# Thin products of the triangular inverses issued in groups of four blocks, with dense products between them

## The chip, the cores and the metric

The kernel runs on one core of a Trainium2 chip. A core has engines that run beside each other, each through its own queue in order: TensorE (PE in the profile; its weight loads are shown apart as PEld), VectorE (DVE), ScalarE (ACT), GpSimd (POOL) and SyncE (SP), which here issues the DMA transfers. The metric is the device time of one execution in microseconds (us), lower is better.

## What is computed

One inference step of a hybrid layer for 1024 prompt tokens and 8 sample tokens with 1024 channels, in float32. The input is normed and projected; two token mixers run on slices of that projection; their results are merged through gates, and a SwiGLU block and a per-layer embedding follow. Cut to what matters here:

```python
u = rmsnorm(h, norm_mix)
proj = u @ w_in                               # the dense products of the first half
# mixer 1, RWKV-7: 8 heads, a state of 64 x 64 each, token by token
sa = einsum('bhvk,bhk->bhv', S, a_t)
S = S * w_t + sa[..., None] * b_t + v_t[..., None] * k_t
# mixer 2, gated DeltaNet: 4 heads, in chunks of 64 tokens
lmat = where(strict, einsum('nbhik,nbhjk->nbhij', kb, k) * decay, 0.0)
tinv = triangular_solve(eye + lmat, eye, lower=True, unit_diagonal=True)
v_new = tinv @ vb - (tinv @ (kb * exp(gc))) @ S
# afterwards
mix = gate_a * (o_a @ w_branch_a) + gate_b * (o_b @ w_branch_b)
h = h + mix @ w_out                           # then SwiGLU, the embedding, the final norm
```

The kernel runs both mixers in chunks of 64 tokens, so that both need inverses of unit triangular 64x64 blocks.

## The kernel before

**Dense products.** A weight is split into a rounded part and a rest (`wh`, `wl`: `weights`, L181; ACT rounds at L188, POOL takes the rest at L189), the activations too (`xh`, `xl`; later `oah`, `oal`, `obh`, `obl`), and each product is the sum of three: `wh*xh + wh*xl + wl*xh`. Tokens are cut into three blocks of 344, so a dense product has 128x128 weights and 344 columns. The input projection has 3360 of them (46 column tiles of 72 products, and one narrow one of 48). They come from the generator `stream` (L396), one at a time; ACT takes each finished accumulation off at L432 and SP stores it at L433.

**The order on TensorE** is written out by a planner, `order` (L112). It keeps a clock of its own, which `mm` (L74) advances by an assumed time for each product (a dense one 0.148 us, a thin one of 32 columns 0.058 us). Each piece of other work is a generator (`Task`) that yields a time by which its next products have to stand back, or marks for which they wait. In every round the first task that may go on does; when none may, one dense product of the stream is issued. When the stream is empty, the planner's clock jumps and tasks follow each other with nothing between. The other engines are ordered by the framework's scheduler.

**Thin products.** DVE inverts the 32x32 diagonal blocks; TensorE then makes the corner of each 64x64 inverse from them by two products with 32x32 weights and 32 columns. For RWKV (`rwkv_inverse`, L749) this happens eight times (4 pairs of heads, 2 halves of the prompt), with 16 blocks each: 16 products into `s` from `inv`, GM (L797), ACT copies them (L798), then 16 more from GM, `inv` (L802). Then the `chains` (L817) go on: a recurrence whose products (`c<-PB`, `zp<-X`, `zp<-Rz`) each wait for DVE. For DeltaNet (`inverses`, L1103) it happens once, after a long stretch on DVE (to L1131, for which the task stands back 54.0 us of the planner's clock), with 32 blocks of 128: `f<-AN` and `f<-tm` for the two diagonal pairs (0, 1) and (2, 3), then `f<-LT` of both pairs, and `f<-W` (L1137 to L1156), and last eight groups with 64x64 blocks. A float32 product of this kind shows as two records in the trace.

**What follows.** `steps`, `preps` and `posts` run the DeltaNet recurrence in 8 steps, again with dense products between. The last `post` scales `ob` (L1372), turns it on TensorE (`f<-cs,ob`), DVE multiplies it with the gate (L1380), and SP stores it to `ob_d` (L1381). Behind that store in SP's queue stand the loads of the first branch's input (`U<-oa_d`, L1401), which ACT and DVE split (L239, L240) for the first dense products of the next stage (`acc<-oah`). What is left of the stream is issued there (`order([], dense_in, [])`).

Of the kernel before, what the change touches and what calls it, by code (L numbers as in the profile page):

```python
# [19 lines left out]
P = 128  # L20
T = 1024
NS = 8
TOK = T + NS
NBLK = 3
BW = TOK // NBLK
# [8 lines left out]
EPS = 1e-6  # L34
# [24 lines left out]
def hybrid(ctx, tc, a, o):  # L59
# [4 lines left out]
    done = {}  # L64
    clock = [0.0]
    last = [None]
    ORDER = mybir.DependencyInfo(mybir.DependencyClass.NoSync, mybir.DependencyReason.DATA)

    def late(i):
        """Keeps an instruction behind the products traced so far, so that what it waits for is there when it is issued."""  # L70
        tc.add_manual_dep(i.ins, last[0].name, ORDER, reason="behind the products so far")
        return i

    def mm(out, w, x, start, stop):  # L74
        last[0] = TE.matmul(out, w, x, start=start, stop=stop).ins  # L75
        clock[0] += math.prod(x.shape[1:]) * (0.00042 if x.dtype == F32R else 0.0017) + 0.004
# [8 lines left out]
    class Task:  # L85
        """A generator that yields where its next products have to wait: for so long, or for marks and so long after."""

# [24 lines left out]
    def order(tasks, stream, until):  # L112
        """Traces the products of all tasks in the order in which they are to run, until those of until are done: the
        first task that can go on does, else the stream of dense products. With no tasks: the rest of the stream."""
        until = list(until)
        with tc.manual_schedule(engines={mybir.EngineType.PE}):
            if not tasks:
                for _ in stream:
                    pass
            while until:  # L120
                times = [t.ready() for t in tasks]
                t = next((t for t, r in zip(tasks, times) if r is not None and r <= clock[0]), None)
                if t is not None:
                    if not t.advance():
                        tasks.remove(t)
                        if t in until:
                            until.remove(t)
                elif next(stream, None) is None:
                    clock[0] = min(r for r in times if r is not None)
# [13 lines left out]
    def ft(shape):  # L143
        return psf.tile(shape, F32, tag="f", name="f")
# [55 lines left out]
    def dense(src, nk, xh, xl, evac):  # L200
        """Products with one column tile of a weight; what is at hand of other work goes first."""
        tc.cur_priority += LATER
        wh, wl = weights(src, nk)
        tc.cur_priority -= LATER
        products(wh, wl, nk, xh, xl, evac)
# [20 lines left out]
    def rsq(out, x, scale, eps, m, t):  # L226
        """out = (x * scale + eps)^-0.5; m, t: temporaries. Seed from the exponent, three Newton steps."""
        if x is not None:
            ts(m, x, scale, eps, MULT, ADD)
        ts(t.bitcast(I32), m.bitcast(I32), 1, None, ALU.logical_shift_right)  # L230
        ts(out.bitcast(I32), t.bitcast(I32), -1, 0x5F3759DF, MULT, ADD)
        for _ in range(3):
            tt(t, out, out, MULT)  # L233
            stt(t, t, -0.5, m, MULT, MULT)  # L234
            stt(out, t, 1.5, out, ADD, MULT)
# [8 lines left out]

    # ------------------------------------------------------------------ input norm, per-layer projection
    xstk = ExitStack()
# [11 lines left out]
    def inv_rms(R, ps, pl_, newps):  # L258
        """R = (mean + EPS)^-0.5 from the sums ps, both [P, BW] and the same on all partitions.

        The sums are taken to tokens on partitions, where there is little to compute, and the result is spread again."""
        n = ps.shape[1]
# [17 lines left out]
    with tc.tile_pool(name="ld", bufs=1, side="right", reuse_waits="tile") as ld, \  # L280
# [35 lines left out]
        def sums(g):  # L316
            """The sums of squares of one block; the squares take the place of what is split."""
            sq = (pv + [own], wv + [own], pv)[g]
# [10 lines left out]
            ps = ct([P, BW])  # L329
# [66 lines left out]
    def stream(jobs):  # L396
        """The products of the input projection, one tile of its columns after the other; yields after each product."""
        def fetch(ti):
# [54 lines left out]
    def conv(ci):  # L453
        """Short causal convolution of one tile of q, k, v, by blocks of tokens; 2 silu of it goes to c_d."""
        w = [vc("conv", j * 12 + ci) for j in range(4)]
# [47 lines left out]

    # ------------------------------------------------------------------ RWKV-7
    lstk, rstk = ExitStack(), ExitStack()
# [39 lines left out]
    def shifted(ti, raw, dst=None):  # L545
        """raw: [P, TOK + 1], column 0 the zero before the prompt; token shift, in place or to dst (chunks, samples)."""
        late(G.tensor_copy(sho[:, ti], raw[:, T:TOK + 1]))
# [161 lines left out]
    def gram(F, hf):  # L709
        """Products within the chunks of one half."""  # L710
        v, BC, KR, cvf = (F[x] for x in ("v", "BC", "KR", "cv"))
# [37 lines left out]
    def rwkv_inverse(f, hf):  # L749
        """The inverses of the triangular blocks."""  # L750
        GM = UT[f, hf]["GM"]
# [44 lines left out]
        for b in range(16):  # L796
            mm(ps[32:64, b], GM[0:32, b, 32:64], inv[0:32, b], start=True, stop=True)  # L797
        act(E, ps[32:64], AF.Copy)  # L798
        yield 1.0
        ps = st1([P, 16, 32])  # L800
        for b in range(16):
            mm(ps[0:32, b], E[:, b], GM[32:64, b, 32:64], start=True, stop=True)  # L802
        act(GM[0:32, :, 32:64], ps[0:32], AF.Copy)
        mark(("inverse", f, hf), 1.0)

    YT = {}

# [92 lines left out]
    def rwkv_sample(f, sm):  # L900
        """One step for the eight samples; partitions (head, value), free (sample, key)."""
        sm, sn = sm
# [51 lines left out]
    def branch_in(f):  # L954
        """The input of the first branch: the normed rows and the bonus, times the gate."""
        g2 = gsp.tile([P, BW], F32, tag="cu", name="g2", bufs=1)[:, :P]
# [22 lines left out]

    # ------------------------------------------------------------------ gated DeltaNet  # L980
    NB = NM * HB
# [18 lines left out]
    def decays():  # L1000
        """beta, g of all tokens (on partitions), the decay between the tokens of a chunk."""
        yield ("pa", "b"),
# [102 lines left out]
    def inverses():  # L1105
        """The inverses of the triangular blocks of all heads and chunks."""
        for m in range(NM):
# [23 lines left out]
        V.transpose(A2.rearrange("p b c -> p c b"), XT4[qd[2]])  # L1131
        yield 54.0
        PS = {}
        for q0 in (0, 16):
            bs = range(q0, q0 + 16)
            ps = ft([P, 16, 32])
            for (u, w), nat in (((0, 1), AN), ((2, 3), tm4)):  # L1137
                for b in bs:
                    mm(ps[qd[w], b - q0], LTb[qd[u], b, qd[w]], nat[qd[u], b, 0:32], start=True, stop=True)
            E = LB4[:, q0:q0 + 16]  # L1140
            for w in (1, 3):
                act(E[qd[w]], ps[qd[w]], AF.Copy)
        yield 0.9
        for q0 in (0, 16):
            bs = range(q0, q0 + 16)
            E = LB4[:, q0:q0 + 16]
            ps = ft([P, 16, 32])
            for u, w in ((0, 1), (2, 3)):
                for b in bs:
                    mm(ps[qd[u], b - q0], E[qd[w], b - q0], LTb[qd[w], b, qd[w]], start=True, stop=True)  # L1150
                act(LTb[qd[u], q0:q0 + 16, qd[w]], ps[qd[u]], AF.Copy)
            yield 0.9
            ps = ft([P, 16, 32])
            for b in bs:
                mm(ps[qd[1], b - q0], LTb[qd[1], b, qd[1]], E[qd[1], b - q0], start=True, stop=True)
            act(AN[qd[1], q0:q0 + 16, 0:32], ps[qd[1]], AF.Copy)  # L1156
# [18 lines left out]
    def gdn_sample():  # L1175
        """One step for the eight samples; partitions value, free (head, sample, key)."""
        qs_, ks_, vs_, zs_ = (smp[:, i] for i in (0, 0, 2, 3))
# [209 lines left out]

    # ------------------------------------------------------------------ branches and merge
    hU = pool(ctx, "hU", 1, "right")
# [51 lines left out]
    def square(m, b, last=False):  # L1441
        """Sum over the channel tiles of h^2; with the last tile, its mean's inverse root goes to R."""
        c = cols(b)
# [25 lines left out]

    # ------------------------------------------------------------------ SwiGLU, per-layer embedding, final norm  # L1470
    hstk = ExitStack()
# [75 lines left out]
def layout(i):  # L1547
    """The inputs in the order in which the chip reads them (transposed, cut into tiles, concatenated)."""
    i = {k: np.asarray(v) for k, v in i.items()}
# [59 lines left out]
```

## Time and profile before

| | us |
|---|---|
| median of three runs | 2112.76 |
| the three runs | 2109.33, 2112.76, 2114.94 |
| span of the profiled execution, first to last instruction | 2108.4 |
| TensorE busy in it | 1970.4 |

The profiled execution's own time is not listed apart from its span; the span lies 0.9 us under the fastest run and 4.4 us under the median. The page cuts the span into 40 slices with the busy share of each engine and TensorE's granted clock; queries give stretches, waits and single instructions. Matmuls are pipelined: the duration of one dense product (0.32 us) is twice the spacing from one start to the next, so costs are taken here from starts.

### The profile page before, as it was taken

To read this page: it belongs to the slowest core of one execution; us is meant where nothing else is said; L and a number is where in the kernel's file an instruction comes from. 1 tells how busy PE (TensorE), PEld (TensorE's weight loads), DVE (VectorE), ACT (ScalarE), POOL (GpSimd) and SP (SyncE) were. 2 spreads that over 40 slices of the span, in tenths; PEclk is the share of its full clock that TensorE was granted. 3 is DMA by queue.
4 is the path that set the end of the run, shared out by engine and by line. 5 is a ranking of instruction groups with operands and counts; after the bars stand their busy time and mean duration, and the time that the engine had idled before them with its cause. 6 is when DMAs were issued, how large, how long until landed. Compare 5 with 4: busy or idle time off the path is not lost.

```text
span 2108.4 us, 35962 instructions
## 1 busy us (share of the span) xinstructions
PE 1970.4 (93%) x13440; PEld 1872.5 (89%) x13440; DVE 1125.4 (53%) x2889; ACT 729.5 (35%) x1785; POOL 875.2 (42%) x1019
## 2 busy tenths in 40 slices
PE   6997899888898999798999999999999999999996
PEld 5987778777787879688999999999999999999995
DVE  8459757889988749727545352221222122223567
ACT  5334344455554442136623332211221121123442
POOL 5366343356464344533027433323322332333642
PEclk9998899999999999789999999999999999999998
DMA  6433233133233434554464311111111111111232
GB/s 220 131 111 110 80 96 102 56 113 102 90 113 100 140 91 138 148 154 133 135 193 135 97 54 51 46 40 57 46 41 45 55 47 38 54 49 41 67 100 97
DMA packets 171048, 195.67 MB, mean 93 GB/s; under 512 B 42968, under 2 KB 130920, under 8 KB 170872
## 3 DMA queue, kind: packets, MB, share of 16 engines
q1 hardware_dynamic: 170872, 193.36, 30.2%
q8 instruction: 106, 1.74, 0.3%
q14 instruction: 70, 0.57, 0.1%
HBM read 141.26 MB, written 52.03 MB: 92 GB/s over the span
## 4 chain that ended last, share of the span: by engine, by line
PE 52%; DVE 1%; ACT 0%; issue 0%; DVEq 0%; ACTq 0%
PE acc L75 50%; PE f L75 1%; PE x L75 1%; PE o L75 0%; PE f L79 0%; DVE fo L1529 0%; DVE U L1517 0%; DVEq L1595 0%; DVE b L1514 0%; DVE nrr L234 0%; DVE nrr L233 0%; ACT jk L1292 0%; ACT R L278 0%; DVE b L1516 0%; ACT t L1335 0%
## 5 line engine op out<-in xcount | busy, mean ns | idle before, releaser
L189 POOL TENSOR_TENSOR wl<-ws,wh 128x512 fp32r<-128x512 f32 (+2 forms) x292 | 365.1, 1266 | 645.4 <-ACT wh L188 629.1
L75 PE MATMUL acc<-uxh,wh 128*128 128x344 f32 (+2 forms) x1248 | 400.3, 321 | 0.1
L75 PE MATMUL acc<-uxl,wh 128*128 128x344 f32 (+2 forms) x1248 | 399.5, 320 | 0.0
L75 PE MATMUL acc<-uxh,wl 128*128 128x344 f32 (+2 forms) x1248 | 399.5, 320 | 0.0
L75 PE MATMUL acc<-xh,wh 128*128 128x344 f32 (+1 forms) x1128 | 388.5, 344 | 3.6 <-ACT gs L432 3.6
L75 PE MATMUL acc<-xl,wh 128*128 128x344 f32 (+1 forms) x1128 | 384.5, 341 | 1.8 <-DVE xl L243 1.8
L75 PE MATMUL acc<-xh,wl 128*128 128x344 f32 x1104 | 379.4, 344 | 0.0
L188 ACT ACTIVATE wh<-ws 128x512 fp32r<-128x512 f32 (+2 forms) x292 | 161.6, 595 | 415.7 <-PE acc L75 376.6
L75 PEld LDWEIGHTS acc<-uxh,wh 128*128 128x128 f32 x1248 | 234.9, 188 | 1.0 <-DVE b L1514 0.4
L75 PEld LDWEIGHTS acc<-uxh,wl 128*128 128x128 f32 x1248 | 234.9, 188 | 0.6
L75 PEld LDWEIGHTS acc<-uxl,wh 128*128 128x128 f32 x1248 | 234.3, 188 | 0.7
L75 PEld LDWEIGHTS acc<-xh,wh 128*128 128x128 f32 (+1 forms) x1128 | 220.3, 195 | 11.8 <-ACT gs L432 3.9
L75 PEld LDWEIGHTS acc<-xl,wh 128*128 128x128 f32 (+1 forms) x1128 | 220.7, 196 | 9.8 <-DVE xl L243 2.4
L75 PEld LDWEIGHTS acc<-xh,wl 128*128 128x128 f32 x1104 | 218.3, 198 | 5.6 <-issue 0.9
L75 PE MATMUL acc<-hidl,wh 128*128 128x344 f32 x528 | 169.3, 321 | 0.0
L75 PE MATMUL acc<-hidh,wh 128*128 128x344 f32 x528 | 169.2, 321 | 0.0
L75 PE MATMUL acc<-hidh,wl 128*128 128x344 f32 x528 | 168.8, 320 | 0.0
L1494 DVE TENSOR_TENSOR U<-U,acc 128x344 f32<-128x344 f32 x96 | 49.3, 513 | 160.4 <-PE acc L75 159.7
L1481 DVE TENSOR_TENSOR a<-acc,R 128x344 f32<-128x344 f32 x66 | 34.1, 517 | 179.5 <-PE acc L75 169.5
L1489 DVE TENSOR_TENSOR a<-acc,sgt 128x344 f32<-128x344 f32 x66 | 34.0, 516 | 161.3 <-PE acc L75 161.3
L1483 POOL TENSOR_TENSOR sgt<-sgt,R 128x344 f32<-128x344 f32 x66 | 61.2, 927 | 103.8 <-ACT sgt L1482 103.8
L75 PEld LDWEIGHTS acc<-hidl,wh 128*128 128x128 f32 x528 | 99.3, 188 | 0.0
(470 smaller groups left out, 3765.5 us busy)
## 6 DMA issues: line engine op xcount, KB each, us to landing
ws<-in_win SPq DMA_DIRECT2D x92, 256.0 KB, 2.8
pa_d<-gs SPq DMA_DIRECT2D x90, 172.0 KB, 1.9
ws<-in_wg SPq DMA_DIRECT2D x44, 256.0 KB, 2.6
ws<-in_wu SPq DMA_DIRECT2D x44, 256.0 KB
gate_d<-gs SPq DMA_DIRECT2D x48, 172.0 KB, 2.5
a<-gate_d SPq DMA_DIRECT2D x48, 172.0 KB, 2.5
ws<-in_wd SPq DMA_DIRECT2D x32, 256.0 KB, 2.7
c_d<-cy SPq DMA_DIRECT2D x36, 172.0 KB, 1.9
```

What stands on the lines that cost most here:

```text
L75: last[0] = TE.matmul(out, w, x, start=start, stop=stop).ins
L188: act(h[:, k], s, AF.Copy)
L189: gtt(l[:, k], s, h[:, k].bitcast(F32), SUB)
L1481: tt(y, ps, R[:, c], MULT)
L1483: gtt(sgt[:, c], sgt[:, c], R[:, c], MULT)
L1489: tt(y, ps, sgt[:, c], MULT)
L1494: tt(U[m][:, cols(b)], U[m][:, cols(b)], ps, ADD)
```

## The change

Two things move on TensorE. In `rwkv_inverse`, after every fourth of the 16 thin products the task now yields THIN = 0.44 us of the planner's clock, which is three dense products if no other task wants to go on. In `inverses`, a helper `thin` does the same, and where there are two diagonal pairs it issues both products of a block next to each other instead of 16 of one pair and then 16 of the other. There the two ACT copies (L1151 before) come after both. Besides, the DeltaNet inverses stand back 62.0 instead of 54.0 us. No product is added or removed; docstrings and comments were cleared.

```diff
@@ rwkv_inverse
         for b in range(16):
             mm(ps[32:64, b], GM[0:32, b, 32:64], inv[0:32, b], start=True, stop=True)
+            if b % 4 == 3 and b < 15:
+                yield THIN
         act(E, ps[32:64], AF.Copy)
         yield 1.0
         ps = st1([P, 16, 32])
         for b in range(16):
             mm(ps[0:32, b], E[:, b], GM[32:64, b, 32:64], start=True, stop=True)
+            if b % 4 == 3 and b < 15:
+                yield THIN
+    THIN = 0.44
@@ inverses
-        yield 54.0
+        yield 62.0
+        def thin(bs, products):
+            for b in bs:
+                for p in products:
+                    p(b)
+                if b % 4 == 3 and b < bs[-1]:
+                    yield THIN
...
-            for (u, w), nat in (((0, 1), AN), ((2, 3), tm4)):
-                for b in bs:
-                    mm(ps[qd[w], b - q0], LTb[qd[u], b, qd[w]], nat[qd[u], b, 0:32], start=True, stop=True)
+            yield from thin(bs, [lambda b, u=u, w=w, nat=nat, ps=ps: mm(
+                ps[qd[w], b - q0], LTb[qd[u], b, qd[w]], nat[qd[u], b, 0:32], start=True, stop=True)
+                for (u, w), nat in (((0, 1), AN), ((2, 3), tm4))])
...
+            yield from thin(bs, [lambda b, u=u, w=w, E=E, ps=ps: mm(
+                ps[qd[u], b - q0], E[qd[w], b - q0], LTb[qd[w], b, qd[w]], start=True, stop=True)
+                for u, w in ((0, 1), (2, 3))])
             for u, w in ((0, 1), (2, 3)):
-                for b in bs:
-                    mm(ps[qd[u], b - q0], E[qd[w], b - q0], LTb[qd[w], b, qd[w]], start=True, stop=True)
                 act(LTb[qd[u], q0:q0 + 16, qd[w]], ps[qd[u]], AF.Copy)
             yield 0.9
             ps = ft([P, 16, 32])
-            for b in bs:
-                mm(ps[qd[1], b - q0], LTb[qd[1], b, qd[1]], E[qd[1], b - q0], start=True, stop=True)
+            yield from thin(bs, [lambda b, E=E, ps=ps: mm(
+                ps[qd[1], b - q0], LTb[qd[1], b, qd[1]], E[qd[1], b - q0], start=True, stop=True)])
```

TensorE's queue at the third of the eight RWKV inverses, before (`acc<-x..` are dense products of the input projection, `s` the thin ones, `zp` and `c` the chain):

```order
L75 MATMUL acc<-xh_105,wh 128x344
L75 MATMUL s<-inv,GM 32x32 x16
L75 MATMUL zp<-X,GM 64x64 x2
L75 MATMUL acc<-xl_113,wh 128x344
L75 MATMUL acc<-xh_105,wl 128x344
L75 MATMUL acc<-xh_106,wh 128x344
L75 MATMUL acc<-xl_114,wh 128x344
L75 MATMUL acc<-xh_106,wl 128x344
L75 MATMUL acc<-xh_107,wh 128x344
L75 MATMUL s<-GM,inv 32x32 x16
```

And in the changed kernel, the first 16 of the same inverse:

```order
L75 MATMUL s<-inv,GM 32x32 x4
L75 MATMUL zp<-X,GM 64x64 x2
L75 MATMUL acc<-xh_104,wh 128x344
L75 MATMUL acc<-xl_112,wh 128x344
L75 MATMUL s<-inv,GM 32x32 x4
L75 MATMUL acc<-xh_104,wl 128x344
L75 MATMUL acc<-xh_105,wh 128x344
L75 MATMUL acc<-xl_113,wh 128x344
L75 MATMUL s<-inv,GM 32x32 x4
L75 MATMUL acc<-xh_105,wl 128x344
L75 MATMUL acc<-xh_106,wh 128x344
```

One run of 16 became four runs of 4; over the whole RWKV part 17 unbroken runs of thin products became 64.

TensorE's queue at the start of the DeltaNet inverses, before (`AN` and `tm` hold what DVE made ready for the pairs (0, 1) and (2, 3)):

```order
L75 MATMUL acc<-xh_102,wl 128x344
L75 MATMUL f<-AN,LT 32x32 x16
L75 MATMUL f<-tm_9028,LT 32x32 x16
L75 MATMUL f<-AN,LT 32x32 x16
L75 MATMUL f<-tm_9028,LT 32x32 x16
L75 MATMUL acc<-xh_103,wh 128x344
L75 MATMUL acc<-xl_111,wh 128x344
```

And in the changed kernel:

```order
L75 MATMUL acc<-xl_112,wh 128x344
L75 MATMUL f<-AN,LT 32x32
L75 MATMUL f<-tm_9094,LT 32x32
L75 MATMUL f<-AN,LT 32x32
L75 MATMUL f<-tm_9094,LT 32x32
L75 MATMUL f<-AN,LT 32x32
L75 MATMUL f<-tm_9094,LT 32x32
L75 MATMUL f<-AN,LT 32x32
L75 MATMUL f<-tm_9094,LT 32x32
L75 MATMUL acc<-xh_104,wl 128x344
L75 MATMUL acc<-xh_105,wh 128x344
L75 MATMUL acc<-xl_113,wh 128x344
```

The two pairs alternate block by block, and three dense products follow each four blocks. From here to the first 64x64 product 4 unbroken runs became 22, and 33 dense products became 82. Counted from the front, 2937 dense products of the stream stand ahead of the first of these thin products before, and 3038 in the changed kernel (47 of the 101 come in the RWKV part, 54 from the 62.0); behind the last 64x64 product 366 are left before, and 212 now.

TensorE's queue at the end of the DeltaNet recurrence, before:

```order
L75 MATMUL acc<-xh_100,wh 128x344
L75 MATMUL acc<-xl_108,wh 128x344
L75 MATMUL x<-x,Kd 128x128 x4
L75 MATMUL o<-x,M 128x128 x4
L75 MATMUL acc<-xh_100,wl 128x344
L75 MATMUL acc<-xh_101,wh 128x344
L75 MATMUL acc<-xl_109,wh 128x344
L75 MATMUL acc<-xh_101,wl 128x344
```

And in the changed kernel:

```order
L75 MATMUL acc<-xh_107,wl 128x344
L75 MATMUL x<-X,LT 128x128 x4
L75 MATMUL x<-x,Kd 128x128 x4
L75 MATMUL o<-x,M 128x128 x4
L79 MATMUL f<-cs,ob 128x128 x8
L75 MATMUL acc<-oah_11754,wh 128x344 x3
L75 MATMUL acc<-oal_11758,wh 128x344
```

Before, 118 dense products of the stream stand between the last `o<-x,M` and the first `acc<-oah`, and 24 more come soon after; now the stream's last product stands ahead of the last step's `x<-X`, and none is left behind it. On SP the loads `U<-oa_d` stand behind the last `ob_d` store in both.

## Rows read from the trace of the kernel before

**Rows 1.** Stretches (us): length, busy time and instructions by engine, granted clock, DMA.

```profile
200.00:740.00 540.00, 476.26 (x3720) 416.71 (x3721) 443.34 (x1344) 253.78 (x613) 256.37 (x388) 0.93 0.33 99
...
1060.00:2060.00 1000.00, 999.82 (x6292) 996.83 (x6291) 311.93 (x606) 246.77 (x498) 371.43 (x339) 1.00 0.22 64
...
203.50:220.00 16.50, 11.95 (x90) 10.93 (x88) 14.81 (x40) 6.71 (x14) 6.22 (x13) 0.50 0.25 77
...
876.00:913.00 37.00, 28.21 (x353) 26.18 (x353) 14.90 (x20) 6.33 (x11) 15.47 (x21) 0.50 0.32 101
...
1030.00:1053.00 23.00, 23.00 (x156) 22.96 (x155) 8.86 (x33) 11.54 (x37) 3.83 (x3) 1.00 0.51 172
```

**Rows 2.** Waits of PE: product, awaited instruction: us in total, times, longest.

```profile
PE c L75 <- DVE PB L849: 25.5, 15, 5.5
PE zp L75 <- DVE X L837: 19.2, 16, 3.0
```

**Rows 3.** Timeline of PE, RWKV thin run at full clock: start us, us, line, product, records.

```profile
502.51 0.32 PE L75 MATMUL acc<-xh,wl 128*128 128x344 f32 x1
502.76 1.19 PE L75 MATMUL s<-GM,inv 32*32 32x32 f32 x32
503.89 0.43 PE L75 MATMUL acc<-xh,wh 128*128 128x344 f32 x1
504.15 0.32 PE L75 MATMUL acc<-xl,wh 128*128 128x344 f32 x1
```

**Rows 4.** One record of such a run: ns shortest/median/longest, first and last start.

```profile
L75 PE MATMUL s<-GM,inv x256: 190/191/254, 211.7 to 727.2; 32*32 32x32 f32 x128
```

**Rows 5.** Timeline of PE, first RWKV inverse (in brackets: idle before, releaser).

```profile
203.04 1.84 PE L75 MATMUL s<-inv,GM 32*32 32x32 f32 x32 [3.15 <-DVE inv L788]
...
211.74 1.88 PE L75 MATMUL s<-GM,inv 32*32 32x32 f32 x32 [4.55 <-DVE GM L792]
```

**Rows 6.** Timeline of PE, DeltaNet inverses.

```profile
872.90 0.32 PE L75 MATMUL acc<-xh,wl 128*128 128x344 f32 x1
881.52 1.91 PE L75 MATMUL f<-AN,LT 32*32 32x32 f32 x32 [8.30 <-DVE AN L1129]
885.35 1.75 PE L75 MATMUL f<-tm,LT 32*32 32x32 f32 x29 [1.92 <-DVE tm L1131]
...
886.97 0.24 PE L75 MATMUL f<-tm,LT 32*32 32x32 f32 x1
887.00 0.24 PE L75 MATMUL f<-AN,LT 32*32 32x32 f32 x1
...
895.12 1.91 PE L75 MATMUL f<-LT,W 32*32 32x32 f32 x32 [0.68 <-ACT LT L1151]
...
897.42 0.49 PE L75 MATMUL acc<-xh,wl 128*128 128x344 f32 x1
897.70 0.49 PE L75 MATMUL acc<-xh,wh 128*128 128x344 f32 x1
...
913.10 1.15 PE L75 MATMUL f<-AN,LT 128*64 128x64 f32 x16
```

**Rows 7.** Timeline of PE, end of the DeltaNet recurrence.

```profile
1032.50 1.06 PE L75 MATMUL o<-x,M 128*128 128x128 f32 x8
...
1052.86 0.47 PE L75 MATMUL acc<-oah,wh 128*128 128x344 f32 x2
```

**Rows 8.** Timeline of ACT, same place.

```profile
1039.16 1.28 ACT L1372 ACTIVATE ob<-ob,so 128x128 f32<-128x128 f32 x4 [1.21 <-DVE so L235]
...
1049.73 1.25 ACT L239 ACTIVATE oah<-U 128x344 fp32r<-128x344 f32 x3 [3.34 <-DMA U<-oa_d]
```

**Rows 9.** Timeline of DVE, same place.

```profile
1044.56 0.75 DVE L1380 SCALAR_TENSOR_TENSOR z<-z,gn,f 128x512 f32<-128x512 f32 x1 [5.50 <-PE f L79]
```

**Rows 10.** Timeline of SP's DMA issues, same place.

```profile
1045.33 0.37 SPq L1381 DMA_DIRECT2D ob_d<-z  x1
1045.80 0.46 SPq L1401 DMA_DIRECT2D U<-oa_d  x1
```

More of the change, by code (lines that the diff above doesn't have):

```diff
@@ L1131, in inverses @@
         V.transpose(A2.rearrange("p b c -> p c b"), XT4[qd[2]])
-        yield 54.0
-        PS = {}
+        yield 62.0
[5 more added lines that the diff above has]
+                    yield THIN
         for q0 in (0, 16):
```

## The prediction

> **What bounds the kernel now.** I read the stretches first. From 1060 to 2060 us TensorE is busy 999.8 of 1000 us at full clock [rows 1]: dense products follow each other without a gap, 6292 of them, so one costs 0.159 us, and whatever is saved or lost earlier moves this part as a whole. Everything in question lies in the first half. There the same dense products serve as filling: the stream has a fixed number, so a product that is issued earlier is not cost, but it is gone as filling later. I therefore count each stretch as its time less 0.159 us for each dense product in it, call that the excess, and ask at the end where the stream runs dry.
>
> Second, the waits: in the RWKV part (200 to 740 us, TensorE busy 476 of 540 us, VectorE 443) the chain's products wait 25.5 + 19.2 us in 31 pieces [rows 1, 2]. Third, the timeline at the thin products. In the RWKV part a run of 32 records goes at full clock (1.19 us), and only the first inverse waits for VectorE, 3.15 and 4.55 us [rows 3, 5]; the clock is at half (0.50, the lower level of 1.2 GHz) from there to 220 us [rows 1]. At the DeltaNet inverses TensorE waits 8.30 and then 1.92 us for VectorE, and 0.68 us twice for ScalarE; from 876 to 913 us the clock is at half throughout, and there a run of 32 records takes 1.91 us and dense products stand 0.28 us apart [rows 1, 6].
>
> **What a run costs beside its records.** At full clock a dense product starts at 502.51, the run at 502.76, the next dense product at 503.89 and the one after at 504.15 [rows 3]. That is 1.64 us, less two dense products 1.32. The records are (1.19 - 0.19)/31 = 0.032 us apart, the 0.19 being one record's own length [rows 3, 4], 1.03 us for 32. So going into a run and out of it costs 0.29 us, however short the run is. The bounds are 0.2 (part of the late second dense product is not the run's) and 0.4 (at the lower clock). The Trainium skill (TensorEngine Tiling (Array Packing), Key Properties) says that a change of tiling mode drains TensorE, names no price, and so speaks against cutting runs; the trace agrees, and with no such price the sum below would be 18.8 us lower.
>
> **The RWKV part.** 17 runs become 64: 47 x 0.29 = 13.6 us more. Against that, three things. The second wait of the first inverse: 9 more dense products and three more switches stand ahead of it, at the lower clock 9 x 0.28 + 3 x 0.4 = 3.7 us, and the first stage's own pace adds a little, so I take 4.0 of the 4.55 us as gone; the first wait of 3.15 stays, nothing is put ahead of it. With that hole filled the clock should return some 7 us sooner; about half the work done in them is then saved, 3 us (0 to 5). Last, the chain's waits: its hops get 13.6 us of switches and 47 x 0.159 = 7.5 us of dense products more between them, 21 us over eight inverses, while VectorE works at its own pace, so waits that come from VectorE being late shrink. Between none (the waits stand where nothing was put in) and all 21 I take a third, 7, since the hops around the inverses are about a third of all. Sum: 13.6 - 4.0 - 3.0 - 7.0 = -0.4 us, bounds -14 to +8.
>
> **The DeltaNet inverses.** Before: from the end of the last dense product's slot (872.90 + 0.16) to the first 64x64 product at 913.10 [rows 6], 40.0 us with 33 dense products, an excess of 34.8.
> After: the 54 more dense products that the 62.0 lets out take 8.6 us and TensorE arrives at 881.6, when `AN` is there (881.52). But now each block's second product needs `tm`, ready at 885.35 [rows 6], so of 8.30 + 1.92 us a wait of 3.9 is left (1 to 7: VectorE's queue also holds the sample step's work, which shifts). The 0.68 us waits go, since both pairs now stand ahead of the copies.
> Records: 256 alternate between two pairs. The trace has a few such neighbours by accident, where two runs overlap: 886.97 and 887.00, 0.03 us apart, at half clock, where one pair alone goes at (1.91 - 0.24)/31 = 0.054 [rows 6]. I take 0.030, 7.7 us, and 64 x 0.032 = 2.1 us for the rest. The bounds at full clock are 0.016 (half of 0.032) and 0.032. By the Trainium skill (TensorE: Matmul & The Clock Gate, Part 3, The mechanism) tiles on other row groups start about 4 ns apart, so that a second pair would be nearly free; the half-clock row agrees, no row shows it at full clock, and the sum by it would be some 3.6 us lower.
> Runs: 22 x 0.29 = 6.4 us. Clock: after the 3.9 us wait I expect a short stretch at 1.2 GHz as after the other waits, then full clock with three dense products to each group; 2.5 us (0 to 13).
> Excess after: 3.9 + 7.7 + 2.1 + 6.4 + 2.5 = 22.6. Change -12.2 us, bounds -18 to -2.
>
> **The end of the recurrence.** By order, 154 dense products more of the stream are issued by then (47 + 54 + 49 from the runs, 4 from neighbours). Before, 118 stand between the last `o<-x,M` and the first `acc<-oah`, and TensorE is busy all of 1030 to 1053 us [rows 1]. Now none is left, and TensorE stands in what they hid. That chain, from the end of `o<-x,M` (1032.50 + 1.06 [rows 7]): norm and scaling of `ob` to 1040.44, 6.9 us [rows 8]; turns 0.4 (VectorE's idle time ends on them); gate 0.75 [rows 9]; two issues on SP, 1045.33 to 1045.80, 0.47 [rows 10]; the load until the split starts at 1049.73, 3.93 [rows 8]; a third of the three splits, 0.42. Together 12.9 us, in which TensorE has 0.7 us of work: 12.2 idle. The last step's own hops lose their 8 dense products, 1.2. After so long a pause the first dense products run at the lower clock, some 14 x 0.12 = 1.7. Sum +15.1, bounds +10 (SP and ScalarE, with less to do, are quicker) and +20 (weights for the next tiles queue behind eight splits on ScalarE). Nothing hides this: TensorE's next work is what waits.
>
> **Sum.** -0.4 - 12.2 + 15.1 = +2.5 us. The trace's own span of 2108.4 would become 2111; set against the median of 2112.76, 2115. I call 0.3% (6.3 us) what a measurement can tell from no change.
>
> **Rivals.**
> 1. *The clock stays low in the DeltaNet stretch* (slower). If three dense products to a group don't bring full clock back, 82 dense products cost 0.12 us more each, 9.8 us, and the 64 single records 1.4; with the 2.5 already counted, +8.7, so 2124. For it: 33 dense products among the runs did not lift the clock before [rows 1, 6]. Against: runs of 32 records with four dense products between them go at full clock in the RWKV part [rows 3]. It decides if the clock is still at half some 7 us after `tm` came.
> 2. *The end costs more* (slower): at +20 the time is 2120. It decides if `acc<-oah` starts over 16 us after the last `o<-x,M`.
> 3. *The chain gives way* (faster): VectorE is late because it is behind, and nearly all 21 us go into waits that exist anyway, 44.7 us of them [rows 2], with fewer falls of the clock after them: another -12, 2103. For it: both engines have idle time in that part [rows 1]. Against: the waits are few and short near the thin runs.
> 4. *The loads come earlier* (faster): should `U<-oa_d` not stand behind the last store in time, the end costs 5, and the time is 2105.
> 5. *The change does nothing at the pairs*: at 0.032 us a record they cost 8.3 instead of 7.7; within the forecast.
>
> **How the numbers follow.** Forecast, gain and loss about equal: 0.45, its own range 2107 to 2122, of which 0.37 lies within 0.3% and 0.08 above it. Rival 1: 0.15, rival 2: 0.10, rival 3: 0.25, rival 4: 0.05. So faster 0.30, same 0.37, slower 0.33. The range reaches to rivals 1 and 3 and past them by some of the unknown: 2100 to 2127.
>
> **What would show it.** Right: TensorE's wait for `AN` gone and one for `tm` of about 4 us; the stretch of the thin DeltaNet products at full clock for the most part; dense products right before and after a thin group 0.25 us apart; a hole of about 12 us ahead of the first `acc<-oah`, with a fall of the clock; the waits of the chain at 35 to 45 us in total. Wrong: a hole there of under 6 us, chain waits under 30 us, or half clock through the DeltaNet stretch.

## The result and the profile after

The changed kernel takes 2126.16 us in the median of four runs (2121.36 to 2130.11) beside 2113.2 for the kernel before on the same chip (2109.33 to 2114.94), a ratio of 1.0062 [1.0041, 1.0084]; ten later runs give 1.0031 [1.0006, 1.0055]. It is slower by 8 to 13 us in the medians (8.2 in the ten later runs). The forecast was 2115, its range 2100 to 2127: the first median is inside the range by 1 us, on the side that had a chance of 0.33, and 11 us from the forecast. The profiled execution has a span of 2119.6 us, 11.2 more than before, and belongs to the fastest of the four.

The stretches of it that answer to [rows 1] (columns as there): the RWKV part, the DeltaNet inverses, the end of the recurrence, the dense part.

```profile
200.00:740.00 540.00, 480.94 (x3555) 412.73 (x3555) 420.83 (x1291) 247.52 (x591) 253.77 (x384) 0.91 0.30 92
...
905.00:945.00 40.00, 35.29 (x436) 27.66 (x436) 9.33 (x28) 9.00 (x17) 27.00 (x35) 0.83 0.58 156
...
1049.00:1068.00 19.00, 7.18 (x43) 5.79 (x43) 10.32 (x37) 9.00 (x37) 1.27 (x1) 0.70 0.56 182
1084.00:2084.00 1000.00, 999.90 (x6313) 996.63 (x6312) 314.64 (x622) 247.14 (x499) 370.01 (x338) 1.00 0.20 62
```

The dense part is what it was, 1000 us without a gap. The DeltaNet inverses stand at 0.83 of the clock instead of 0.50. At the end of the recurrence, where TensorE was busy all the time, it is busy 7.18 of 19 us. Its waits over the whole span, those that bear on this (us in total, times, longest):

```profile
PE zp L75 <- DVE X L842: 31.7, 18, 5.4
PE c L75 <- DVE PB L854: 14.8, 11, 3.6
...
PE acc L75 <- ACT oah L239: 6.9, 1, 6.9
...
PE acc L75 <- ACT gs L432: 6.0, 4, 3.0
...
PE f L79 <- ACT ob L1386: 4.4, 1, 4.4
PE f L75 <- DVE y L974: 4.1, 1, 4.1
...
PE s L75 <- DVE inv L788: 3.8, 1, 3.8
...
PE s L75 <- DVE GM L792: 1.7, 1, 1.7
```

The chain's two waits come to 46.5 us where they were 44.7 [rows 2]. The waits for `AN` and `tm` [rows 6] are gone. New are those for `oah` and `ob` at the end of the recurrence, which nothing hides now, and the one for `y`; the waits for `gs` came to 3.6 us before.

In the table every stretch is its time less 0.159 us for each dense product that the order puts into it, less the same of the kernel before: the excess of the prediction. The stretches end at the last `f<-kc`, the first `x<-S`, the last `x<-S` and the span's end. "Left" is the number of products of the stream behind the last `x<-S`. The names are those of the experiments below. Each row is one profiled execution; the last column is the median of all runs less that of the kernel before beside it. One execution of rwkv_g8 (2697.16 us at a mean clock of 0.647) was in a slow state; without it the median there is +8.9.

| kernel | RWKV | DeltaNet inverses | recurrence | end | sum | left | median |
|---|---|---|---|---|---|---|---|
| before | 0 | 0 | 0 | 0 | 0 | 154 | 0 |
| changed | +16.5 | -10.7 | -9.5 | +14.9 | +11.2 | 1 | +13.0 |
| after_again | +12.7 | -10.9 | -9.4 | +15.4 | +7.8 | 1 | +8.2 |
| e1_rwkv_groups | +3.4 | -5.3 | -1.9 | +2.7 | -1.1 | 105 | +5.6 |
| e1_again | +18.1 | -5.3 | +1.5 | +1.9 | +16.2 | 105 | +11.3 |
| rwkv_g8 | +10.5 | -5.6 | +1.9 | -0.3 | +6.5 | 146 | +9.4 |
| sixth_not | +15.1 | -3.4 | -7.1 | +2.5 | +7.1 | 104 | +5.2 |
| sixth_only | -1.6 | +1.2 | -3.2 | +0.5 | -3.1 | 155 | -3.4 |
| e2_pairs_62 | +4.8 | -5.1 | -6.6 | +1.8 | -5.1 | 113 | -9.3 |
| e4_delta_only | +2.0 | -7.8 | -2.8 | +8.5 | -0.1 | 59 | -3.3 |
| wait62 | -0.4 | -7.2 | -6.0 | +1.7 | -11.9 | 113 | -12.6 |
| pairs_54 | +2.0 | -4.4 | -2.8 | +1.3 | -3.9 | 154 | -5.3 |
| wait62_first | +3.0 | -5.2 | -4.5 | +8.4 | +1.7 | 47 | +5.8 |
| e3_late_recurrence | +6.6 | -1.2 | -2.5 | +15.2 | +18.1 | 6 | +14.2 |

Six kernels have the RWKV part of before unchanged (e2, e3, e4, wait62, pairs_54 and before itself): there the column spreads from -0.4 to +6.6. That is what one trace says of this column, and medians are needed beside it. The spread goes with the clock: ordered by this column, the six spend 71.7, 78.5, 81.9, 85.3, 88.7 and 95.6 us of the stretch from 200 to 850 us at half clock.

The next column is no clean reading of the DeltaNet part either. In six traces (both of the RWKV groups, rwkv_g8, sixth_not, sixth_only and e3) the code of the DeltaNet inverses is that of before, and the column runs from -5.6 to +1.2; with groups in several RWKV inverses it is -3.4 to -5.6. In the two traces of the RWKV groups TensorE is idle 12.2 and 12.3 us in that stretch where it was 16.4, with less waiting for `gs`, for `v<-c_d` and for `AN`.

### The profile page after: what moved, and what is told of

Same layout as the page of the kernel before. It is cut to its first block, busy times and chain, and to the rows that moved or that the text cites. A ratio compares the mean times of both kernels' runs of the same rounds, so it can differ in the third digit from the quotient of the medians.

```text
span 2119.6 us, 35989 instructions
## 1 busy us (share of the span) xinstructions
PE 1982.7 (94%) x13440; PEld 1867.4 (88%) x13440; DVE 1117.2 (53%) x2891; ACT 729.7 (34%) x1783; POOL 879.3 (41%) x1019
## 4 chain that ended last, share of the span: by engine, by line
PE 72%; DVE 19%; issue 3%; ACT 2%; DMA 2%; POOL 1%; SPq 0%; DVEq 0%; POOLq 0%; ACTq 0%
PE acc L75 63%; PE f L75 3%; PE c L75 2%; PE zp L75 2%; PE s L75 1%; DVE GM L732 1%; DVE inv L768 1%; PE f L79 1%; DVE inv L769 1%; DVE L L621 1%; DVE LB L790 1%; PE x L75 1%; DVE cy L484 0%; DVE inv L770 0%; DVE LB L756 0%
## 5 line engine op out<-in xcount | busy, mean ns | idle before, releaser
L482 POOL TENSOR_TENSOR cy<-cy,cu 128x344 f32<-128x344 f32 x72 | 70.3, 976 | 83.4 <-ACT cu L481 82.5
```

The source lines that it names most:

```text
L482: gtt(y, y, u, ADD)
```

## The experiments

**The parts of the change.** First the RWKV groups alone (`if b % 4 == 3 and b < 15: yield 0.44` in both loops of `rwkv_inverse`):

> The RWKV part of the change alone: its thin products in groups of four with a dense product between (47 more thin runs), the DeltaNet inverses as before. Theory from the profile of the changed kernel (its RWKV stretch gained 16.5 us over the 7.5 us of its 47 dense products): +13 to +20 us over the kernel before, about 2129. Rival 1, the prediction's sum (runs paid by shorter chain waits and an earlier clock): -5 to +5 us. Rival 2, the 16.5 us are the runs' switch cost alone, 47 x 0.29: +13 to +14 us, and the count of low-clock stretches between 200 and 760 us stays at the 21 pieces of before; under the theory with the clock in it, it rises to about 28. The end of the recurrence: only 47 dense products are issued earlier, about a third of the changed kernel's 154 in the inverses plus 47, so its last phase keeps most of its cover.

2118.69 us beside 2113.06, ratio 1.0031 [1.0011, 1.0051]: +5.6, between the theory and rival 1. Its profile fell on the fastest of ten executions (2109.09); its low-clock pieces, counted as in the expectation, are the 21 of before, as rival 2 had them.

The pairs and the later start, without groups:

```diff
-        yield 54.0
+        yield 62.0
...
-            for (u, w), nat in (((0, 1), AN), ((2, 3), tm4)):
-                for b in bs:
-                    mm(...)
+            for b in bs:
+                for (u, w), nat in (((0, 1), AN), ((2, 3), tm4)):
+                    mm(...)
```

> The DeltaNet inverses with pairs side by side and the later start of their last stage (62 instead of 54), without groups there, and the RWKV inverses as before. Theory: the later start takes the wait for the transposed blocks (8.30 us) and the pairs halve the spacing of the thin records, while 54 or so more dense products spent there use up slack and leave some cover for the end of the recurrence: -8 to -14 us, about 2101. Rival 1, the clock still falls in one long thin run after the filling: -2 to +2 us. Rival 2, the cover at the end of the recurrence is lost already with these dense products: +3 to +8 us, with a hole of 10 us or more between the last state product and the first attention product.

2103.73, ratio 0.9955 [0.9938, 0.9972]: -9.3, as the theory had it, and 1.8 us at the end.

The order alone:

```diff
     # ahead of the recurrence's first preparation, prep(0)
+        yield 23.0
```

> Order alone: the kernel before with the recurrence held back by 23 (in the planner's time, some 145 dense products issued ahead of it instead of in it and behind it). No thin product, pair or group differs. Theory: dense products issued earlier leave none to cover the end of the recurrence, +15 us there, and the recurrence with its operands long finished waits less, -9.5 us: sum +4 to +8 us, about 2119. Rival 1, the hole at the end of the changed kernel comes from the thin products' order and not from the count of dense products left: -9 to +1 us, no hole of 10 us. Rival 2, the recurrence gains nothing by starting later: +13 to +17 us.

2127.29, ratio 1.0062 [1.0037, 1.0086]: +14.2, rival 2. The end costs its 15 us and the recurrence hardly gains. Its waits there (timeline of TensorE):

```profile
1064.85 1.35 PE L79 MATMUL f<-cs,ob 128*128 128x128 f32 x4 [4.28 <-ACT ob L1373]
1071.87 1.23 PE L75 MATMUL acc<-oah,wh 128*128 128x344 f32 x3 [5.67 <-ACT oah L239]
```

They are those of the changed kernel:

```profile
1053.07 1.02 PE L79 MATMUL f<-cs,ob 128*128 128x128 f32 x4
1058.52 1.35 PE L79 MATMUL f<-cs,ob 128*128 128x128 f32 x4 [4.43 <-ACT ob L1386]
1066.77 1.23 PE L75 MATMUL acc<-oah,wh 128*128 128x344 f32 x3 [6.89 <-ACT oah L239]
```

No thin product differs in this experiment, so the hole comes from how the dense products are spread, and not from the thin ones.

The DeltaNet part entire (e2 with the groups as well):

> The whole DeltaNet part of the change (groups of four, pairs side by side, the start at 62), the RWKV inverses as before. Theory, the profile of the changed kernel by stretches: inverses -10.7, recurrence -9.5, end of it between 0 and +15 (47 dense products fewer are gone by then than in the changed kernel): -20 to -5 us, about 2100 if most of the cover is left, 2108 if none is. Rival, the cover costs as much as in the changed kernel and the recurrence gains nothing without the RWKV part: +2 to +6 us. If this kernel and the one with the RWKV groups alone add up to the changed kernel (+13), the parts are independent.

2109.73, ratio 0.9981 [0.9964, 0.9999]: -3.3, between the theory and its rival. Against e2 (the pairs and the start at 62) the groups cost 6.0 us; the end alone makes 6.7: 59 products are left instead of 113, which cover the turn of `ob` but not the load behind it.

```profile
1054.28 1.23 PE L75 MATMUL acc<-oah,wh 128*128 128x344 f32 x3 [5.90 <-ACT oah L239]
```

**The whole again, and single pieces.**

> The changed kernel, unaltered, for a second trace and more times beside the same runs of the kernel before. The parts measured apart come to +5.6 (RWKV groups) and -3.3 (DeltaNet part), sum +2.3 us, and the kernel as a whole to +13. Theory A, the parts meet at the end of the recurrence (one dense product left there against 105 and 59 in the parts): the end costs +15 again, the parts' ends cost +2.7 and +8.5, so the whole is 4 us more than the sum, about +6, and the rest of the first +13 was the clock's chance in the RWKV stretch (30 low pieces there against 22 to 28 in five other traces); a second trace then shows 22 to 28 and its RWKV stretch ends 5 to 13 us earlier. Theory B, the RWKV stretch of the whole is truly slower (its clock falls more often whenever the groups are there): +11 to +15 again, low pieces 29 or more between 200 and 850 us.

2121.04, ratio 1.0031 [1.0006, 1.0055]: +8.2, between the theories' +6 and +11. The end makes some 4 more of the whole than of the parts (15 against 2.7 + 8.5), as theory A had it. Its sum of the medians is not settled by this: the parts alone come to +2.3 with the first run of the RWKV groups and to +8 with the second (below), so 4 more make +6 or +12. The low pieces, counted as in the expectation, are 25, which is theory A's 22 to 28. But the RWKV column is +12.7 here, 3.8 below the first trace and not the 5 to 13 that theory A asked for, and the long stretch at half clock is there again, from 581 us: that much of theory B stands.

The RWKV products in groups of eight (`b % 8 == 7` for `b % 4 == 3`):

> The RWKV products in groups of eight, 16 more thin runs instead of 47, the rest as before. Theory, a price per run (5.6 us for 47 runs, 0.12 each): +2 us (-1 to +5). Rival, the cost comes from the chain being moved by dense products in its inverses at all and not from the number of runs: +5 us as with 47 runs. Rival, the switch price that the trace of before shows, 0.29 a run, with nothing given back: +4.6 us here and +13.6 with 47 runs (which that run did not give).

2122.28, ratio 1.0047 [1.0031, 1.0063]: +9.4 for what are 15 more runs in TensorE's queue (32 where there were 17). Neither price per run gives that, 0.12 or 0.29; it costs as much as 47 more runs, which gave +5.6 here and +11.3 below.

The start at 62 alone, and the pairs alone:

> The later start of the last DeltaNet inverse stage alone (62 for 54): no pairs, no groups. Theory, the start takes the wait for the transposed blocks (8.30 us, of which 8 dense products at 0.159 are no excess): -3 to -5 us, so about half of the -9.3 us of start and pairs together; the thin stretch stays at the low clock. Rival, the start gives nothing since the next wait takes its place: -1 to +1 us; then the pairs alone carry the gain.

> Pairs side by side alone, the last inverse stage starting at 54 as before. Theory, the pairs halve the spacing of 320 paired records (from the profile of the changed kernel 0.06 a pair at the low clock, 0.032 at the full clock, against 0.11 and 0.06 a pair before): -4 to -7 us, with the wait of 8 us still there. Rival, the gain of start and pairs together (-9.3) is the start's alone: -1 to +1 us here.

The start: 2100.28, ratio 0.9937 [0.9917, 0.9957], -12.6, the best kernel of all and more than twice what was expected. TensorE waits no longer for `AN`; one wait for `tm` is left, and the stretch that follows is still at half clock:

```profile
885.57 1.75 PE L75 MATMUL f<-tm,LT 32*32 32x32 f32 x29 [2.44 <-DVE tm L1131]
```
```profile
885.00:916.00 31.00, 29.08 (x339) 26.49 (x340) 9.17 (x25) 8.08 (x14) 22.43 (x29) 0.51 0.56 158
```

The expectation had taken the dense products that fill the wait out of the gain; they are work that has to be done anyway, so the whole wait is gained: -7.2 in that stretch. The other -6.0 is the recurrence, which nothing in the edit touches. The pairs alone: 2107.62, ratio 0.9963 [0.9942, 0.9983], -5.3, as expected. Together (e2) they give -9.3, not -18: with the thin products issued faster TensorE stands for 3.9 us at the products behind them, for `y`. In its one trace another 4.8 us stand in the RWKV column, whose code is that of before.

**Where the RWKV groups lose.**

> The RWKV groups alone once more, unaltered, as the measure for the next two and for a second trace. Its first trace ended its RWKV stretch 9 to 13 us (in excess) ahead of two traces of the changed kernel with the same instructions in the same order up to there; the one difference is that the clock stayed full at the sixth inverse (584 us), where it fell to half for 24 us in the others. Theory A, that fall is chance and the usual case: a second trace shows it (7 or so low pieces from about 580), and this kernel's usual time is +5 to +9 us. Theory B, the fall needs the DeltaNet part of the change: a full clock again, +3 to +6 us.

2123.30, ratio 1.0050 [1.0026, 1.0074]: +11.3, and the fall is there: theory A, though above its +5 to +9. This series ran on another chip than the first one of this kernel; the kernel before takes 2113.06 and 2111.98 on the two. Same instructions, same order, same wait ahead of the sixth inverse in both executions. But the fall at the sixth inverse is not the one difference, as the expectation has it: the two part before. Both wait 2.2 us for `LB` at 529 us, at half clock. In the first execution half clock lasts from 524.5 to 541.6 us, and TensorE comes to the next product of the chain late enough to wait little:

```profile
545.15 0.44 PE L75 MATMUL zp<-X,GM 64*64 64x64 f32 x4 [1.39 <-DVE X L841]
```

In the second it ends at 535.8 us, TensorE gets ahead and waits longer, and the clock falls again, from 546.1 to 556.3 us:

```profile
546.52 0.69 PE L75 MATMUL zp<-X,GM 64*64 64x64 f32 x4 [4.43 <-DVE X L841]
```

At the sixth inverse the first stayed at full clock:

```profile
583.14 0.44 PE L75 MATMUL zp<-X,GM 64*64 64x64 f32 x4 [2.44 <-DVE X L841]
...
584.09 0.32 PE L75 MATMUL acc<-xl,wh 128*128 128x344 f32 x1
584.35 0.43 PE L75 MATMUL s<-inv,GM 32*32 32x32 f32 x8
584.71 0.43 PE L75 MATMUL acc<-xh,wl 128*128 128x344 f32 x1
584.97 0.32 PE L75 MATMUL acc<-xh,wh 128*128 128x344 f32 x1
```

In the second the clock fell there, and a group of eight records with its three dense products takes 1.72 us (589.09 to 590.81):

```profile
587.03 0.69 PE L75 MATMUL zp<-X,GM 64*64 64x64 f32 x4 [2.43 <-DVE X L841]
...
589.09 0.63 PE L75 MATMUL s<-inv,GM 32*32 32x32 f32 x8
589.65 0.66 PE L75 MATMUL acc<-xh,wl 128*128 128x344 f32 x1
590.11 0.49 PE L75 MATMUL acc<-xh,wh 128*128 128x344 f32 x1
590.39 0.49 PE L75 MATMUL acc<-xl,wh 128*128 128x344 f32 x1
590.81 0.63 PE L75 MATMUL s<-inv,GM 32*32 32x32 f32 x8
```

The excess over the kernel before, at the first and behind the last thin product of the fifth and the sixth inverse and behind the eighth, with the granted clock of 570 to 612 us:

| kernel | fifth | sixth | eighth | clock |
|---|---|---|---|---|
| changed | +0.1, +3.1 | +12.4, +19.9 | +17.4 | 0.72 |
| after_again | -3.8, -0.7 | +8.4, +15.9 | +13.5 | 0.72 |
| e1_again | +1.3, +4.3 | +13.7, +21.2 | +19.0 | 0.76 |
| e1_rwkv_groups | +1.0, +4.0 | +9.0, +10.5 | +4.3 | 1.00 |
| sixth_not | 0.0, +3.0 | +12.2, +13.7 | +18.4 | 0.84 |
| wait62 | -1.5, -1.5 | +1.5, +0.6 | -0.6 | 0.96 |

Of these, wait62 has no groups. A grouped inverse costs 2.3 to 3.0 us in itself at full clock (second to fifth, in the trace of e1_rwkv_groups), and where the fifth starts nearly all of it has come back (-3.8 to +1.3), as the prediction had it. Then it fails: 5 to 9 us are lost between the fifth inverse and the sixth, and 7.5 in a grouped sixth where the clock has fallen (1.5 where it is full). So the next two kernels took the sixth apart.

```diff
-            if b % 4 == 3 and b < 15:
+            if b % 4 == 3 and b < 15 and (f, hf) != (2, 1):    # sixth_not; sixth_only: == (2, 1)
```

> RWKV groups of four in seven of the eight inverses; the sixth (the one at 584 us) in unbroken runs of 16 as in the kernel before. The count of dense products issued up to the end of the RWKV stretch is the same within one as with all eight. Theory A, the cost of the RWKV groups is mainly the long stretch at half clock in the sixth inverse: 6 to 12 us less than with all eight, -4 to +1 us beside the kernel before, and 2 or 3 low pieces between 570 and 612 us instead of 7. Theory B, the price per thin run: 6 of 47 runs fewer, 1 us less than with all eight.

2117.17, ratio 1.0020 [1.0007, 1.0032]: 6.1 less than with all eight in the same series, as theory A had it, but still +5.2 over before. Across the sixth inverse its trace loses 1.5 instead of 7.5, though the clock falls there too, for 13.6 us (585.2 to 598.8), four low pieces where theory A asked for 2 or 3. The 9 us ahead of it are lost all the same, and it drifts up behind it where the others come back.

> Groups of four in the sixth RWKV inverse alone, everything else as before; the dense products issued up to the end of the RWKV stretch are as many as before, within one. Theory A, the long stretch at half clock comes with the groups of this inverse: +5 to +10 us for six runs more. Theory B, a price per run: +0.7 us (0.12 each, by the groups in all) or +1.7 us (0.29 each). Theory C, the clock falls there only after the waits as the five grouped inverses ahead leave them: -1 to +2 us and no more low pieces at 575 to 610 us than before (3).

2108.57, ratio 0.9993 [0.9975, 1.0010]: no difference, theory C. The clock is full at 570 to 612 us. The groups in this inverse alone do no harm; the loss ahead of it comes with what stands in front. With groups in the first five inverses the clock falls a second time at 540 to 546 us (in three of the four traces with all groups, and in sixth_not), at a wait for `X` of 4.43 us that was 2.14.

That loss does not need groups. The last kernel below, wait62_first, has none, only its first inverse moved, and its trace loses 9.2 us between the fifth and the sixth inverse, with a wait for `X` of 6.79 us:

```profile
546.40 0.68 PE L75 MATMUL zp<-X,GM 64*64 64x64 f32 x4 [6.79 <-DVE X L837]
```

Over all traces: six have a wait for `X` of 4.43 to 6.79 us there, and lose 6.5 to 9.4 us in this stretch against before; in the other eight the longest is 1.39 to 2.58 us, and the loss 0.0 to 5.0. So it goes with the chain out of step and a second fall of the clock, whatever moved the chain. Why it comes out of step there and not at the first four inverses is not settled.

**A better kernel from this?**

```diff
-        yield 34.0                                 # rwkv_inverse, ahead of its products, on top of wait62
+        yield 34.0 if f or hf else 38.0
...
-        yield 1.0
+        yield 1.0 if f or hf else 6.0
```

> The later start of the DeltaNet stage alone (62), and later starts of the first RWKV inverse's two products (38 for 34, 6 for 1), so that dense products fill its waits of 3.15 and 4.55 us. It issues 58 more dense products before the recurrence and leaves 47 behind it, where the start of 62 alone leaves 113. Theory, by the runs so far the phase behind the recurrence costs +1.8 us with 113 left and +8.5 with 59, so 47 cost about +10: the waits (7.7 us and some 4 us of half clock) are paid back by 8 us of the end, -2 to -5 us beside the start of 62 alone, so -15 to -18 us beside the kernel before. Rival 1, the filled waits only move the chain of the RWKV states and come back as its waits: -3 to -7 us beside the kernel before. Rival 2, no cover lost at the end: -19 to -23 us.

2117.76, ratio 1.0024 [1.0008, 1.0040]: +5.8, worse than any expected. The waits at the first inverse vanish (a new one of 3.65 us for `gs` stands between its two products), and the excess is -3.8 us behind it and -6.0 behind the fifth. Then 9.2 us are lost ahead of the sixth, and the RWKV column ends at +3.0. The chain starts later and waits more for `X` and less for `PB`, 47.5 us together for 44.7:

```profile
PE zp L75 <- DVE X L837: 33.1, 20, 6.8
PE c L75 <- DVE PB L849: 14.4, 9, 5.0
```

They were 19.2 and 25.5 [rows 2]. The end of the recurrence costs 8.4 with 47 products left, so rival 1 and the theory's own end add up. The best kernel stays the one with the single number changed, 62 for 54.

## Why the prediction was right or wrong

- *TensorE as the bound, and the excess as the measure*: held. All but about 1 us of +11.2 stands ahead of the dense part.
- *0.29 us a run*: held in rows that the kernel before could not give. In the trace of e1_rwkv_groups, from the dense product at 584.09 to the second behind the group at 584.97 is 0.88 us; less two dense products 0.56, less eight records at 0.034 (0.43 less 0.19, over seven), 0.29.
- *RWKV, -0.4*: this term failed, and the step in it is the repayment of 14 us. The changed kernel's traces show +16.5 and +12.7, and in the five traces with groups of four in seven or eight inverses the median is +15.1 where unchanged code shows about +2. The cost of 13.6 is, if anything, low: at full clock each grouped inverse costs 2.3 to 3.0 us from its first to its last thin product, where six runs at 0.29 make 1.7. The three repayments did not come. The second wait of the first inverse gave 2.9 of the 4.0 (4.55 to 1.7), but the first grew by 0.7. The clock did not come back sooner: 0.50 for 17 us from 203 us as before. And the chain's waits did not shrink by 7 us: they are 46.5 and 45.0 us in the two traces where they were 44.7. From the span's start to the last `f<-kc` TensorE is idle 93.6 and 90.0 us (94.2 before), and at half clock 116.1 and 119.5 us (99.0 before). My reading, which no run here shows by itself: what is put between two hops covers a wait, but it also delays the chain's next product, for which VectorE's next step waits. The repayment is seen up to the fifth inverse and is lost from there. The upper bound of +8 was too low, since it left out that the clock can stay at half through a grouped inverse (+7.5, where one at full clock costs 1.5 to 3.0). The one trace of all groups without the falls at 540 to 546 us and at the sixth inverse, e1_rwkv_groups, is inside the bounds: idle 7.1 us less than before, and +3.4.
- *DeltaNet inverses, -12.2*: near in number, -10.7 and -10.9, with other pieces, and in part by luck: the DeltaNet part alone gives -7.8 (e4), inside the bounds, and the RWKV groups alone, with this code untouched, -5.3. The wait for `AN` is gone and the clock mostly full. There is no wait for `tm`, because TensorE came late: four waits for `gs` (6.0 us) held the dense products ahead. Without the RWKV groups it is there, 3.60 us in e2 and 2.53 in e4, as the prediction's 3.9 had it. A wait of 4.14 for `y` was not foreseen: a thin product needs the PSUM tile that VectorE has still to empty, behind reductions that wait for GpSimd (6.32 and 2.40 us for `st`). And the pairs were cheaper than the 0.030 a record that was taken.

TensorE's timeline there, from the last wait for `gs` to the third group:

```profile
904.96 0.42 PE L75 MATMUL acc<-xh,wh 128*128 128x344 f32 x1 [3.02 <-ACT gs L432]
...
909.85 0.21 PE L75 MATMUL f<-AN,LT 32*32 32x32 f32 x1
909.85 0.21 PE L75 MATMUL f<-tm,LT 32*32 32x32 f32 x1
...
910.09 0.19 PE L75 MATMUL f<-AN,LT 32*32 32x32 f32 x1
910.10 0.19 PE L75 MATMUL f<-tm,LT 32*32 32x32 f32 x1
910.22 0.42 PE L75 MATMUL acc<-xh,wl 128*128 128x344 f32 x1
910.48 0.32 PE L75 MATMUL acc<-xh,wh 128*128 128x344 f32 x1
...
922.37 0.64 PE L75 MATMUL f<-LT,W 32*32 32x32 f32 x16 [4.14 <-DVE y L974]
```

Sixteen records start within 0.25 us, 0.017 from one to the next. The two of a pair start 0.00 to 0.01 us apart. The Trainium skill (TensorE: Matmul & The Clock Gate, Part 3, The mechanism) has tiles on other row groups start about 4 ns apart, and the trace now agrees at full clock; the sum by it, 3.6 us lower, was the better one for this piece.

- *The end, +15.1*: right in size and in mechanism. +14.9 and +15.4; idle 4.43 + 6.89 + 0.50 = 11.8 us against 12.2. The order alone makes it (e3), and the table gives the curve: 146 to 155 products left cost -0.3 to 1.3, 104 to 113 cost 1.7 to 2.7, 59 and 47 cost 8.5 and 8.4, 6 and fewer 15.
- *The recurrence*: the sum had no term for it, and it gave -9.5 and -9.4, most of what the RWKV term lost. TensorE's waits in it fall from 8.2 us to 1.1, and a fall of the clock at 968 us is gone. That it starts later is not reason enough: e3 starts as late and gains 2.5. Other kernels show between -7.1 and +1.9. What decides it was not tried.
- *The rivals*: the clock did come back in the DeltaNet stretch (1), the end did not cost 20 (2), the chain gave nothing (3), the loads came no earlier (4), and the pairs cost less and not more than the forecast took (5). The sign that was named for "wrong", chain waits under 30 us, pointed to the other side only; the one that mattered, chain waits above 45, was not priced.

So the nearness of +2.5 to +8 and +11 is part luck: one term as forecast by its mechanism (the end), one near by number (the DeltaNet inverses), one off by 13 to 17 and one of -9.5 left out, which went the other way.

## What to carry to other kernels

Filling that comes from a stream of fixed length is a budget. Count what is left of it at the last place that needs it: here about 100 of 3360 products decide 15 us. The RWKV groups, the later start and the pairs cost that place 1.3 to 2.7 us each when they stand alone, and with the DeltaNet groups they met there. And an insertion into a dependent chain is not paid back merely because the chain's waits are as long as it is: whether it hits the engine that waits or delays the one that is waited for has to be followed hop by hop. Where the clock can fall or not, several executions of the same kernel are needed, and the place where they first part is to be looked for, which can lie well ahead of the place where the loss shows.

## What the runs showed of the hardware

After the same wait of 2.43 to 2.45 us at the same instruction, the clock was granted in full in one execution with all RWKV groups and fell to half in three others. The four had the same instructions up to there, but the three had gone through another wait and fall of the clock some 40 us earlier, so what decides it is not shown. With thin groups and three dense products between them the clock then stayed at half for 20 to 24 us, and with unbroken thin runs, after the same history and a wait of 2.44 us, for 13.6 (sixth_not); the two falls of the kernel before near this place (575 and 606 us) last 6.8 and 3.4. Sixteen 32x32 records on two pairs of quadrants start 0.017 us apart at full clock and 0.027 at half (908.19 to 908.60), where one pair alone has 0.032 and 0.054 between its records, so a second pair is all but free at either level.
